# The RWKV-7 loop of a hybrid backbone, rewritten as a pipeline over units with TensorE in program order

## Chip, cores and metric

One core of a Trainium2 chip. The metric is the device time of one execution of the whole program in microseconds, the median of the runs. The program computes two layers; the change lies in the recurrent branch of the second one, in the last third of the time.

## What is computed

Odd layers mix tokens with a bidirectional RWKV-7 recurrence beside a Hyena convolution. For each of 8 heads a 64x64 state is carried over the 256 context tokens and then the 1024 latent ones, once forwards and once backwards; the two outputs are added, normalised per head, and given a bonus term.

```python
def step(s, inp):
    r_t, w_t, k_t, v_t, kk_t, b_t = inp
    sa = jnp.einsum('bhij,bhj->bhi', s, kk_t)
    s = s * w_t[:, :, None, :] - sa[..., None] * b_t[:, :, None, :] + v_t[..., None] * k_t[:, :, None, :]
    y = jnp.einsum('bhij,bhj->bhi', s, r_t) if emit else None
    return s, y
...
for d in range(2):
    s_ctx, yc = wkv_scan(s0, rc, decay_c, k_c, vc, kkc, b_c, reverse, ctx_out)
    _, yl = wkv_scan(s_ctx, r, decay_l, k_l, v, kk, b_l, reverse, True)
```

All operands are float32, and so are the products in the part that changes.

## The kernel before

The token loop is replaced by blocks of 64 tokens. A **job** is a pair of heads in one direction (4 pairs, 2 directions: 8 jobs). A job has 5 **units** of 256 tokens, the first of them context, so there are 40 units, taken in one order. In a unit there are 4 blocks of 64 tokens for each of 2 heads, and the work on one unit has these stages:

- the **front** (`rw_front`, L1462): loads, sums of log decays (`cs_ps`), exponentials, the keys `AKR` and `BK`, the Gram products `g_ps`, their masked parts `la` (the triangle to be inverted) and `gm` (the part for the outputs), transposes of the keys (`bk_ps`, evicted as `BT`) and the right-hand sides (`rh_ps`, evicted as `R`);
- the **inversion** of the 32x32 diagonal blocks of the triangles (`rw_invert`, L1569), one job at a time (the first job in two pieces) on VectorE: 31 steps of two instructions, `tmp<-L,X` and `X<-X,tmp`. `la` goes there through DRAM, and the result comes back as `XT`;
- the **solve** (`rw_solve`, L1599): three products of four 128x128 matmuls in a chain, `y_ps`, `z_ps`, `w_ps`, with an eviction behind each (`Z` on ScalarE, `R` on VectorE, `At` and `UV` on ScalarE);
- the **transitions** (`rw_trans`, L1629): 16 products of 64x64 (`ph_ps`), evicted by VectorE as `PH` and `RT`;
- the **scan** (`rw_scan`, L1653): 4 blocks one behind the other. Each adds `UV,BT` and the old state times `PH` in `st_ps`, evicts the new state `S` on ScalarE with the decay as its factor, copies the old state into a block-diagonal 128x128 tile, and makes outputs `yo_ps`;
- for the backward units with latent tokens, the bonus term and the **readout** (`rw_bonus`, `rw_readout`).

`rwkv` (L1370) goes through units b = 0 to 39. Fronts run up to 12 units ahead, solves two, transitions one. `PACE` sets how many inversion steps are traced between the others, at a high priority. The list of a loop turn is not the order in which engines work: the instructions are put in order for each engine by a scheduler, which may place any ready matmul on TensorE between two others. `Ordered` (L146) can make TensorE keep the order of the program; here it is off in this loop. From unit 28 on, `Final` projects the finished rows with the output weights (`fe_ps`), four of whose eight row blocks (4 to 7) come from the Hyena branch, and the weights are scaled and split into two parts when they are needed.

Of the kernel before, what the change touches and what calls it, by code (L numbers as in the profile page):

```python
# [10 lines left out]
F32 = mybir.dt.float32  # L11
# [18 lines left out]
def constants():  # L30
    c = {}
# [43 lines left out]
    gm[0, :, 0], gm[0, :, 1] = tc_ > sr, tc_ >= sr  # L75
    gm[1, :, 0], gm[1, :, 1] = tc_ < sr, tc_ <= sr
# [43 lines left out]
FB = 2  # L120
PB = (1, 1, 1, 1, 1)
# [7 lines left out]
PACE = (5,3,3,3)  # L129

NX = 3
XA = 0
# [41 lines left out]
class K:  # L174
# [879 lines left out]
    def gemm3(self, x):  # L1054
# [3 lines left out]
        with ExitStack() as st:  # L1058
# [175 lines left out]
            for n in range(4):  # L1234
                rw(n * 128, n, False, self.wnext(), 0)
                for _ in range(FG[n]):
                    self.rw_next_front()

    def rw_init(self):
# [3 lines left out]
        self.ep = self.fst.enter_context(tc.tile_pool(name="rwe", bufs=5, side="right", reuse_waits="tile"))  # L1243
# [3 lines left out]
        self.rpa = self.pst.enter_context(tc.tile_pool(name="rwpa", bufs=1, side="right", space=PSUM, reuse_waits="tile"))  # L1247
        self.jobs = [(j, d) for j in range(4) for d in range(2)]
        self.seq = [[0, 1, 2, 3, 4], [0, 4, 3, 2, 1]]
        self.fr, self.nf, self.inv = {}, 0, []  # L1250
        C = self.C = {}
        tri = fp.tile([128, 2, 256], F32, name="tri0", tag="kkf", bufs=2)
        nc.sync.dma_start(out=tri, in_=a["k_tri"].rearrange("d p k -> p d k"))
        C["tri"] = fp.tile([128, 2, 256], F32R, name="tri", bufs=1)
        nc.vector.tensor_copy(out=C["tri"], in_=tri)
        C["gm"] = fp.tile([128, 2, 128], F32, name="gm", bufs=1)
        nc.sync.dma_start(out=C["gm"], in_=a["k_gmask"].rearrange("d p k -> p d k"))
        C["LO"] = [[self.ep.tile([128, 4, 128], F32, name=f"LO0{i}", tag="LO0", bufs=5) for i in range(5)]]
        for t in C["LO"][0]:
            nc.vector.memset(t, 0.0)  # L1260
# [9 lines left out]
    def rw_inv(self, n):  # L1270
        while self.inv and n:
            n -= 1
            with self.tc.high_priority(1000):
                if next(self.inv[0], 1):
                    self.inv.pop(0)

    def rw_next_front(self):
        k, i = divmod(self.nf, 5)
        j, d = self.jobs[k]
        if i == 0:  # L1280
            self.fr[k] = self.rw_start(j, d, k)
        with self.tc.issue_after(self.table.ins):
            self.rw_front(self.fr[k], self.seq[d][i], *((self.ep, 5) if self.nf % 12 < 5 else (self.wp, 7)))
# [4 lines left out]
        self.nf += 1  # L1288
# [81 lines left out]
    def rwkv(self):  # L1370
        nc, tc, a = self.nc, self.tc, self.a
        with ExitStack() as st:
            kp = st.enter_context(tc.tile_pool(name="rwk", bufs=1, reuse_waits="tile"))
            pp = st.enter_context(tc.tile_pool(name="rwp", bufs=1, space=PSUM, reuse_waits="tile"))
            wp = st.enter_context(tc.tile_pool(name="rww", bufs=2, reuse_waits="tile"))
            self.rpb, self.wp = pp, wp
# [3 lines left out]
            for n, t in enumerate(C["XT"]):  # L1380
# [4 lines left out]
            C["LO"].append([kp.tile([128, 4, 128], F32, name=f"LO1{i}") for i in range(5)])  # L1385
            C["S"] = [kp.tile([128, 128], F32, name=f"S{i}") for i in range(4)]
            self.ns = 0
            jobs, seq, fr = self.jobs, self.seq, self.fr

            done = {"x": 0, "s": 0, "t": 0}  # L1390
            invert = self.rw_inv

            def fronts(n):
                while self.nf < min(n, 40):
                    invert(PACE[0])
                    self.rw_next_front()
                    if self.nf == 10:
                        for t in C["S"]:
                            nc.vector.memset(t, 0.0)

            def upto(what, n):
                while done[what] < min(n, 40):
                    m = done[what]
                    k, i = divmod(m, 5)
                    j, d = jobs[k]
                    q = seq[d][i]
                    if what == "x":
                        if i == 0:
                            invert(99)
# [747 lines left out]
```

## Time and profile before

| | us |
|---|---|
| median of 3 runs (2471.17 to 2472.86) | 2472.54 |
| the profiled execution | 2487.22 |
| its span, first to last instruction | 2485.4 |

The profile gives the time for which each engine was busy (PE is TensorE, DVE VectorE, ACT ScalarE, POOL GpSimd, SP the queue that issues DMAs), the granted TensorE clock, and rows for groups of instructions or for single runs of them in order of time. A line such as L158 can be that of a helper; the tiles' names tell which product is meant. Matmuls overlap, so the length of a matmul row includes a tail in which the next one of the same shape already runs. The shape before the operands' sizes, as in 64*64, is the part of the 128x128 array that an instruction uses. A float32 matmul stands in the trace as two instructions.

### The profile page before, as it was taken

What the parts mean: (1) busy time and instruction counts of PE and PEld (TensorE: products, weight loads), DVE (VectorE), ACT (ScalarE), POOL (GpSimd) and SP (SyncE); (2) the same over time, 40 slices, a digit from 0 to 9 for tenths busy, and PEclk for the clock granted to TensorE, in tenths of its full rate; (3) what the DMA queues carried; (4) which work ended last, traced back from release to release, by engine and by line L of the source; (5) the groups of instructions that cost most, each with busy time, mean ns of one, the idle gap of its engine ahead of it and who ended that gap; (6) DMA issues with size and microseconds to landing.
All of it is one profiled execution on the core that took longest, in us unless ns stands there. A gap on an engine that the chain in (4) does not pass through costs nothing. (4 is left out here: it accounts for less than half of the span.)

```text
span 2485.4 us, 45290 instructions
## 1 busy us (share of the span) xinstructions
PE 2275.4 (92%) x16647; PEld 1892.6 (76%) x16647; DVE 1568.8 (63%) x3175; ACT 1177.3 (47%) x2695; POOL 931.4 (37%) x959
## 2 busy tenths in 40 slices
PE   4999999999999989779899889999968999998997
PEld 3877888777878877668778778788757877887775
DVE  6255532368667867455486696457797776777425
ACT  5354434456556555532323221366435656665334
POOL 1253235201011654511033244224745464655512
PEclk8999999999999989889999999999858989999999
DMA  8433344682222766843454544574534343444522
GB/s 280 132 123 119 126 147 146 196 254 93 80 68 90 200 199 183 225 165 110 144 164 150 164 158 136 173 257 134 155 85 131 107 122 97 115 134 126 168 73 92
DMA packets 351428, 361.69 MB, mean 146 GB/s; under 512 B 83106, under 2 KB 283055, under 8 KB 350438
## 3 DMA queue, kind: packets, MB, share of 16 engines
q1 hardware_dynamic: 341894, 330.34, 43.5%
q10 hardware_dynamic: 9168, 24.25, 3.2%
q0 software_dynamic: 144, 4.19, 0.4%
q8 instruction: 132, 2.16, 0.4%
q14 instruction: 90, 0.74, 0.1%
HBM read 260.07 MB, written 100.10 MB: 145 GB/s over the span
## 5 line engine op out<-in xcount | busy, mean ns | idle before, releaser
L158 PE MATMUL g_ps<-xl,w_hi 128*128 128x512 f32 x1056 | 268.0, 399 | 1.0 <-ACT w_hi L192 1.0
L158 PEld LDWEIGHTS g_ps<-xl,w_hi 128*128 128x128 f32 x1056 | 198.9, 191 | 44.0 <-issue 1.9
L158 PE MATMUL s_ps<-k,q 128*128 128x256 f32 (+1 forms) x704 | 199.9, 381 | 7.6 <-DVE pn L700 4.3
L441 POOL TENSOR_TENSOR al_acc<-al_acc,al_t 128x512 f32<-128x512 f32 x98 | 129.0, 1316 | 185.6 <-ACT al_t L439 155.5
L196 DVE TENSOR_TENSOR w_lo<-w_raw,w_hi 128x256 fp32r<-128x256 f32 (+1 forms) x184 | 131.2, 769 | 86.6 <-PE g_ps L158 45.3
L187 ACT COPY pt<-pt_ps 128x512 f32<-128x512 f32 (+1 forms) x203 | 102.1, 506 | 139.3 <-PE pt_ps L161 133.7
L1586 DVE TENSOR_TENSOR tmp<-L,X 80x112 f32<-80x112 f32 (+25 forms) x279 | 136.4, 489 | 17.8 <-DMA L<-LD 8.9
L1588 DVE TENSOR_TENSOR X<-X,tmp 80x112 f32<-80x112 f32 (+25 forms) x279 | 140.6, 504 | 6.5
L158 PE MATMUL g_ps<-xl,w_lo 128*128 128x512 f32 x528 | 137.8, 395 | 0.0
L161 PE MATMUL pt_ps<-ident,p 128*128 128x128 f32 x704 | 118.1, 283 | 17.7 <-DVE pt L185 7.5
L158 PE MATMUL g_ps<-xhi,w_hi 128*128 128x512 f32 (+1 forms) x528 | 118.2, 366 | 8.9 <-DVE ac_res L283 4.7
L161 PEld LDWEIGHTS pt_ps<-ident,p 128*128 128x128 f32 x704 | 80.8, 141 | 52.9 <-DVE pt L185 14.8
L158 PEld LDWEIGHTS s_ps<-k,q 128*128 128x128 f32 x704 | 109.9, 200 | 14.6 <-DVE p L700 7.1
L695 ACT ACTIVATE p<-p,mn 128x1280 f32<-128x1280 f32 (+1 forms) x96 | 103.4, 1077 | 35.7 <-DVE p L700 35.5
L439 ACT ACTIVATE al_t<-al_w,condT 128x512 f32<-128x512 f32 x98 | 70.8, 722 | 101.7 <-POOL al_acc L441 60.9
L158 PE MATMUL g_ps<-xhi,w_lo 128*128 128x512 f32 (+1 forms) x528 | 118.2, 362 | 0.0
L881 POOL TENSOR_TENSOR bias<-namask,tt 128x384 f32<-128x384 f32 x64 | 67.5, 1055 | 125.9 <-DVE mn L890 52.0
L158 PEld LDWEIGHTS g_ps<-xl,w_lo 128*128 128x128 f32 x528 | 98.2, 188 | 21.1 <-issue 1.4
L158 PE MATMUL g_ps<-xlo,w_hi 128*128 128x512 f32 (+1 forms) x528 | 112.8, 356 | 0.0
L158 PEld LDWEIGHTS g_ps<-xhi,w_hi 128*128 128x128 f32 x528 | 90.0, 194 | 29.5 <-DVE qraw L549 5.4
L158 PE MATMUL g_ps<-AKR,BK 64*128 64x128 f32 (+1 forms) x640 | 91.1, 335 | 22.6 <-DVE AKR L1505 14.8
L158 PEld LDWEIGHTS g_ps<-xhi,w_lo 128*128 128x128 f32 x528 | 89.0, 189 | 18.9 <-issue 5.8
(438 smaller groups left out, 5869.4 us busy)
## 6 DMA issues: line engine op xcount, KB each, us to landing
w_raw<-rec_w_in SPq DMA_DIRECT2D x33, 512.0 KB
hfw<-FW SPq DMA_DIRECT2D x32, 512.0 KB
w_raw<-attn_w_in SPq DMA_DIRECT2D x13, 1024.0 KB
al_w<-rec_ada_w SPq DMA_DIRECT2D x48, 256.0 KB
tt<-TG SPq DMA_DIRECT2D x64, 192.0 KB
kkf<-KK SPq DMA_DIRECT2D x40, 256.0 KB
q<-qb SPq DMA_DIRECT2D x64, 128.0 KB
HS<-hs SPq DMA_DIRECT2D x32, 256.0 KB
```

Of the source, the lines that this page charges most:

```text
L158: return self.keep(self.pe.matmul(*args, **kw))
L161: return self.keep(self.pe.transpose(*args, **kw))
L187: self.nc.scalar.copy(out=out, in_=in_)
L196: e.tensor_tensor(out=lo, in0=full, in1=hi.bitcast(F32), op=ALU.subtract)
L439: nc.scalar.activation(out=o, in_=wt, func=AF.Copy, scale=self.condT[:, k, ci:ci + 1])
L441: nc.gpsimd.tensor_tensor(out=t, in0=t, in1=o, op=ALU.add)
L695: self.nc.scalar.activation(out=p, in_=p, func=AF.Exp, bias=mn, scale=-1.0, accum_out=rs)
L881: nc.gpsimd.tensor_tensor(out=b, in0=mask, in1=tt, op=ALU.subtract)
L1586: nc.vector.tensor_tensor(out=tv, in0=L[:, s:s + 1, rt].to_broadcast([n, nj, nt]), in1=X[:, rj, s:s + 1].to_broadcast([n, nj, nt]), op=ALU ...
L1588: nc.vector.tensor_tensor(out=X[:, rj, rt], in0=X[:, rj, rt], in1=tv, op=ALU.subtract)
```

## The change

The loop of `rwkv` is written anew, over b = -4 to 39, and `nc.tensor.on = True` keeps TensorE in program order inside it. In turn b, TensorE first works with 128x128 tiles on five different units: the third product of unit b+1 (`rw_solved`), the second of b+2, the first of b+3, then the sums of a front, the key transposes of the front before, and those of unit b+4. Then it works with 64x64 tiles: the four scan steps of unit b, with the halves of a Gram product and the right-hand sides of unit b+4 between the steps; the bonus sum, the transitions of b+1, the readout. Last come the products of `UV` for unit b+1 (`rw_own`), on 128*64 tiles, which now fill the bank `sy_ps` ahead of the scan. The three products of a solve stand in three turns.

Further edits: the Gram products use four 64x64 tiles in place of 64*128 ones; outputs and states are kept as rows of head and token, so the block-diagonal copy of the state is gone, `Y` has another layout, and the bonus and readout products are 64x64; `la` and `gm` become one tile `LG`, masked by two VectorE instructions of 512 elements a row (GpSimd's masking and ScalarE's copy are gone); `AKR` is made by one exponential and one product of 512; of GpSimd's work in a front, one step goes to ScalarE (`kd`) and two products go to VectorE (`kd`, `BK`); LO tiles are filled late, four in all; four PSUM banks rotate for everything but `ph_ps` (two) and `sy_ps` (two); inversion steps have a high priority only ahead of the loop; loads of a front come a turn earlier. `Final` takes its tiles from other places, and its products stand in program order at the end of a turn.

In the order of TensorE this shows within one unit. Before, a stretch of 12 out of 28 rows from one `w_ps` to the next:

```order
L158 MATMUL w_ps<-R,XT_17606 128x128 x4
L161 MATMUL bk_ps<-ident,BK 128x128 x4
L158 MATMUL st_ps<-UV,BT 64x64 x2
L158 MATMUL st_ps<-S,PH 64x64 x2
L161 MATMUL rh_ps<-ident,AKR 128x2x64 x2
L158 MATMUL rh_ps<-V,la 64x64 x8
L158 MATMUL ph_ps<-BT,At 64x64 x2
L158 MATMUL ph_ps<-gm,At 64x64 x2
L158 MATMUL ph_ps<-BT,At 64x64 x2
L158 MATMUL ph_ps<-gm,At 64x64 x2
L158 MATMUL y_ps<-R,XT_17604 128x128 x4
L158 MATMUL cs_ps<-tri,sgs 128x256 x4
```

Now, from one `w_ps` on, the first 12 rows of a turn in the middle of the loop:

```order
L157 MATMUL w_ps<-R,XT_17506 128x128 x4
L157 MATMUL z_ps<-Z,LO_17507 128x128 x4
L157 MATMUL y_ps<-R,XT_17504 128x128 x4
L157 MATMUL cs_ps<-tri,sgs 128x256 x4
L160 MATMUL bk_ps<-ident,BK 128x128 x4
L160 MATMUL rh_ps<-ident,AKR 128x2x64 x2
L157 MATMUL sy_ps<-S,PH 64x64 x2
L157 MATMUL sy_ps<-S,RT 64x64 x2
L157 MATMUL g_ps<-AKR,BK 64x128 x8
L157 MATMUL sy_ps<-S,PH 64x64 x2
L157 MATMUL sy_ps<-S,RT 64x64 x2
L157 MATMUL g_ps<-AKR,BK 64x128 x8
```

The scan steps stood singly between products of other shapes; they now stand together, behind one run of 128x128 products.

On VectorE the inversion steps stand differently against the other work. `R<-R,z_ps` comes once a unit. Before, a stretch between two of them, in the fourth job's inversion:

```order
L1620 TENSOR_TENSOR R<-R,z_ps 128x512
L1649 TENSOR_TENSOR PH<-ident_17610,ph_ps 128x2x2x64
L1651 TENSOR_TENSOR RT<-AKR,ph_ps 128x2x2x64
L1534 TENSOR_TENSOR la<-g_ps,gm 128x256 x2
L1515 TENSOR_TENSOR BK<-af,E 128x2x2x64
L1506 TENSOR_TENSOR AKR<-AKR,kkf 128x2x128
L1586 TENSOR_TENSOR tmp<-L,X 80x31
L1588 TENSOR_TENSOR X<-X,tmp 80x31
L1586 TENSOR_TENSOR tmp<-L,X 80x60
L1588 TENSOR_TENSOR X<-X,tmp 80x2x30
L1620 TENSOR_TENSOR R<-R,z_ps 128x512
```

Now the start of the unit whose first eight steps stand behind `RT` (one step is shown of the eight):

```order
L1697 TENSOR_TENSOR R<-R,z_ps 128x512
L1562 TENSOR_TENSOR BK<-kd,E 128x2x128
L1563 TENSOR_TENSOR BK<-af,E 128x2x2x64
L1554 TENSOR_TENSOR AKR<-AKR,kkr 128x2x128
L1557 TENSOR_TENSOR kd<-kd,kkr 128x256
L1597 TENSOR_TENSOR LG<-g_ps,gm 128x512 x2
L1738 TENSOR_TENSOR PH<-ident_17519,ph_ps 128x2x2x64
L1740 TENSOR_TENSOR RT<-AKR,ph_ps 128x2x2x64
L1655 TENSOR_TENSOR tmp<-L,X 80x31
L1657 TENSOR_TENSOR X<-X,tmp 80x31
```

Before, the 31 steps of a job are spread over four or five units. Now they stand in three units out of five: counted from one `R<-R,z_ps` to the next, ten units hold 8, 16, 7, 0, 0, 10, 15, 6, 0 and 0 steps (62, two jobs), and the products `BK` and `kd` stand behind `R`.

On ScalarE, the copy of the keys `BT` now stands ahead of the first state of a unit:

```order
L1538 ACTIVATE E<-cs_ps 128x256
L1541 ACTIVATE AKR<-cs_ps 128x512
L1545 ACTIVATE Dt<-cs_ps 128x4
L191 CAST sgs<-sg 128x256
L1574 COPY BT<-bk_ps 128x512
L1775 ACTIVATE S<-sy_ps,Dt 128x64
L1556 ACTIVATE kd<-af,oka,vec 128x256
L1775 ACTIVATE S<-sy_ps,Dt 128x64 x2
L1636 COPY R<-rh_ps 128x512
L1775 ACTIVATE S<-sy_ps,Dt 128x64
```

Before, twelve ScalarE instructions of a scan (four evictions and eight copies of half a state) stood between those of other stages.

The diff, cut to what matters here:

```diff
-FB = 2
-PB = (1, 1, 1, 1, 1)
+BANKS = ({"f": 3}, {"f": 4, "p": 1, "y": 2})
-PACE = (5,3,3,3)
-NX = 3
-XA = 0
+PACE = (5, 2, 2, 4)
+NX = 4
+SETS = (5, 8)
...
-    def rw_inv(self, n):
+    def rw_inv(self, n, first=False):
         while self.inv and n:
             n -= 1
-            with self.tc.high_priority(1000):
+            with self.tc.high_priority(1000) if first else ExitStack():
...
+            whole, late = None, None
+            self.rw_inverses(0)
+            self.rw_vectors(0)
+            nc.tensor.on = True
+            for b in range(-4, 40):
+                step, vg = [None] * 4, None
+                if at(b) is not None:
+                    k, i, q = self.rw_unit(b)
+                    j, d = self.jobs[k]
...
+                    step = list(self.rw_scan(b, Y))
+                if at(b + 5) is not None:
+                    self.rw_vectors(b + 5)
+                if at(b + 1) is not None:
+                    self.rw_solved(b + 1)
+                if at(b + 2) is not None:
+                    self.rw_second(b + 2)
+                if at(b + 3) is not None:
+                    self.rw_first(b + 3)
+                if late:
+                    self.rw_stats(*late)
+                self.rw_inv(PACE[1])
+                old, whole = whole, None
+                if self.nl < 40:
+                    self.rw_next_load()
+                if self.nf < 40:
+                    whole = self.rw_next_front()
...
+                    self.rw_turned(self.fr[ko], qo, *pool)
+                    fill = self.rw_gram(self.fr[ko], qo, *pool)
+                if at(b + 4) is not None:
+                    self.rw_keys_turned(b + 4)
+                self.rw_inv(PACE[2])
+                for s in range(4):
+                    if step[s]:
+                        step[s]()
+                    if s < 2:
+                        next(fill, None)
+                    if s == 2 and at(b + 4) is not None:
+                        self.rw_right(b + 4)
...
+                if at(b + 1) is not None:
+                    self.rw_trans(b + 1)
+                if late:
+                    self.rw_readout(*late)
...
+                if b >= 0:
+                    self.rw_outputs(b, Y)
+                self.rw_inv(PACE[3])
+                if at(b + 1) is not None:
+                    self.rw_own(b + 1)
+                if at(b + 4) is not None and b > -4:
+                    self.rw_inverses(b + 4)
...
+                if b >= 28:
+                    F.after(b)
...
+        if lat:
+            nc.vector.tensor_tensor(out=AKR, in0=AKR, in1=kkr[:, 0:2].rearrange("p a (i t) -> p i a t", t=128), op=ALU.mult)
+        else:
+            nc.vector.tensor_tensor(out=AKR[:, :, 1, :], in0=AKR[:, :, 1, :], in1=kv, op=ALU.mult)
-        nc.gpsimd.tensor_scalar(out=kd, in0=v3(af), scalar1=self.col("rwkv_k_a", j), scalar2=C["oka"][:, j:j + 1],
-                                op0=ALU.mult, op1=ALU.add)
-        nc.gpsimd.tensor_tensor(out=kd, in0=kd, in1=kf, op=ALU.mult)
+        nc.scalar.activation(out=kd, in_=v3(af), func=AF.Identity, scale=self.col("rwkv_k_a", j), bias=C["oka"][:, j:j + 1])
+        nc.vector.tensor_tensor(out=kd, in0=kd, in1=kf, op=ALU.mult)
+        nc.vector.tensor_tensor(out=BK[:, :, 64:192], in0=kd, in1=E, op=ALU.mult)
-        self.last_bk = nc.gpsimd.tensor_tensor(out=BK[:, :, 64:192], in0=kd, in1=E, op=ALU.mult)
...
+    def rw_gram(self, F, q, wp, bufs):
+        gp = [self.rps([128, 4, 128], "g_ps") for h in range(2)]
+        for ci in range(4):
+            i, c = divmod(ci, 2)
+            zc = slice(64 * c, 64 * c + 64)
+            for m in range(2):
+                for h in range(2):
+                    z, zo, f0 = slice(64 * h, 64 * h + 64), slice(64 * m, 64 * m + 64), 128 * c + 64 * m
+                    nc.tensor.matmul(gp[h][zo, ci, c0:128], BK[z, i, f0:f0 + 64],
+                                     AKR[z, i, :, zc] if q > 0 else AKR[z, i, 1, zc], start=True, stop=True,
+                                     tile_position=(64 * h, 64 * m))
+            if ci == 1:
+                yield
+        for h in range(2):
+            nc.vector.tensor_tensor(out=LG[:, h, :, c0:128], in0=gp[h][:, :, c0:128],
+                                    in1=mask.unsqueeze(1).to_broadcast([128, 4, 128 - c0]), op=ALU.mult)
...
+    def rw_own(self, n):
+        sy = G["sy"] = self.rps([128, 2, 4, 64], "sy_ps", "y")
+        for ci in range(4):
+            i, c = divmod(ci, 2)
+            for part in range(2 if q > 0 else 1):
+                for h in range(2):
+                    zo = slice(64 * h, 64 * h + 64)
+                    nc.tensor.matmul(sy[zo, part, ci, :], LG[:, h, ci, 0:64] if part else BT[:, ci, zo], UV[:, i, c, h, :],
+                                     start=(ci == 0 and part == 0), stop=False, skip_group_check=True, tile_position=(0, 64 * h))
...
+        def step(ci):
+            i, c = divmod(ci, 2)
+            sy, PH, RT, S = G["sy"], G["PH"], G["RT"], F["S"]
+            if S is not None:
+                for h, zo in heads:
+                    nc.tensor.matmul(sy[zo, 0, ci, :], PH[zo, i, c, :], S[zo], start=False, stop=True, skip_group_check=True,
+                                     tile_position=(64 * h, 64 * h))
+            t = F["S"] = wp.tile([128, 64], F32, name="S", bufs=4)
+            with self.tc.high_priority(60):
+                nc.scalar.activation(out=t, in_=sy[:, 0, ci, :], func=AF.Copy, scale=Dt[:, n0 + ci:n0 + ci + 1])
+            if q > 0:
+                for h, zo in heads:
+                    nc.tensor.matmul(sy[zo, 1, ci, :], RT[zo, i, c, :], S[zo], start=False, stop=True, skip_group_check=True,
+                                     tile_position=(64 * h, 64 * h))
-                for h, zo in heads:
-                    nc.scalar.copy(out=sd[zo, zo], in_=S[zo])
-                nc.tensor.matmul(yp[zc, i, :], RT[:, i, c, :], sd, start=True, stop=False, tile_position=(0, 64 * c))
```

## Rows read from the trace of the kernel before

**Rows 1.** The page: busy time of each engine over the span.

```profile
PE 2275.4 (92%) x16647; PEld 1892.6 (76%) x16647; DVE 1568.8 (63%) x3175; ACT 1177.3 (47%) x2695; POOL 931.4 (37%) x959
```

**Rows 2.** Busy time in stretches; columns: window, length, each engine, clock, DMA.

```profile
core 0: us, PE busy (x) PEld busy (x) DVE busy (x) ACT busy (x) POOL busy (x), PEclk, DMA share, GB/s
1902.30:2255.80 353.50, 341.20 (x3853) 286.62 (x3852) 263.17 (x614) 228.25 (x755) 200.98 (x287) 0.93 0.41 113
2255.80:2455.00 199.20, 190.96 (x1577) 150.19 (x1578) 98.17 (x200) 82.72 (x258) 76.84 (x98) 0.95 0.42 124
1775.00:1860.00 85.00, 61.66 (x418) 50.69 (x415) 77.03 (x163) 36.40 (x112) 50.53 (x63) 0.59 0.37 101
```

**Rows 3.** Timeline of TensorE in one unit: start, length, product, count.

```profile
2201.93 0.33 PE L158 MATMUL st_ps<-S,PH 64*64 64x64 f32 x4
2202.20 0.94 PE L158 MATMUL y_ps<-R,XT 128*128 128x128 f32 x6
...
2205.83 1.16 PE L158 MATMUL z_ps<-Z,LO 128*128 128x128 f32 x8
...
2217.20 0.45 PE L158 MATMUL ph_ps<-BT,At 64*64 64x64 f32 x12
...
2220.91 1.71 PE L158 MATMUL g_ps<-AKR,BK 64*128 64x128 f32 x16
```

**Rows 4.** Groups on ScalarE from 1902.3 to 2255.8: count, busy us, mean ns, idle before.

```profile
L1674 ACT ACTIVATE S<-st_ps,Dt 128x64 f32<-128x64 f32 x105 | 33.2, 316 | 25.9 <-PE st_ps L158 24.1
...
L1554 ACT COPY BT<-bk_ps 128x512 f32<-128x512 f32 x26 | 15.2, 585 | 2.3 <-PE bk_ps L161 0.9 <-PE st_ps L158 0.9
```

**Rows 5.** Groups on VectorE in the same stretch.

```profile
L1588 DVE TENSOR_TENSOR X<-X,tmp 80x231 f32<-80x231 f32 (+15 forms) x166 | 81.8, 493 | 3.5
L1586 DVE TENSOR_TENSOR tmp<-L,X 80x87 f32<-80x87 f32 (+15 forms) x165 | 78.2, 474 | 8.6 <-DMA L<-LD 5.5
L1534 DVE TENSOR_TENSOR la<-g_ps,gm 128x256 f32<-128x256 f32 x50 | 20.7, 415 | 8.0 <-PE g_ps L158 6.6 <-DMA iok<-KK 1.1
L1620 DVE TENSOR_TENSOR R<-R,z_ps 128x512 f32<-128x512 f32 x27 | 18.3, 677 | 9.2 <-PE z_ps L158 9.2
L1515 DVE TENSOR_TENSOR BK<-af,E 128x256 f32<-128x256 f32 x26 | 13.9, 534 | 35.3 <-ACT E L1490 35.3
...
L1649 DVE TENSOR_TENSOR PH<-ident,ph_ps 128x256 f32<-128x256 f32 x27 | 11.1, 410 | 2.0 <-PE ph_ps L158 2.0
```

**Rows 6.** Groups on GpSimd in the same stretch.

```profile
L1538 POOL TENSOR_TENSOR gm<-gm 128x256 f32<-128x256 f32 x42 | 33.7, 804 | 27.4 <-ACT gm L1537 26.6 <-DMA ioa<-AS 0.8
L1517 POOL TENSOR_TENSOR BK<-kd,E 128x256 f32<-128x256 f32 x26 | 26.0, 1001 | 68.4 <-ACT E L1490 38.9 <-issue 27.7 <-PE st_ps L158 1.6
L1508 POOL TENSOR_SCALAR kd<-af,vec,oka 128x256 f32<-128x256 f32 x25 | 22.8, 910 | 1.4
L1510 POOL TENSOR_TENSOR kd<-kd,kkf 128x256 f32<-128x256 f32 x25 | 20.7, 826 | 0.4
```

**Rows 7.** Timeline of VectorE: two inversion instructions with GpSimd idle, then two beside it.

```profile
2101.11 0.37 DVE L1588 TENSOR_TENSOR X<-X,tmp 80x207 f32<-80x207 f32 x1
2101.52 0.35 DVE L1586 TENSOR_TENSOR tmp<-L,X 80x192 f32<-80x192 f32 x1
...
2184.56 0.68 DVE L1588 TENSOR_TENSOR X<-X,tmp 80x112 f32<-80x112 f32 x1
...
2187.47 0.64 DVE L1586 TENSOR_TENSOR tmp<-L,X 80x31 f32<-80x31 f32 x1
```

**Rows 8.** Two idle times of TensorE in its timeline (in brackets, with the releaser).

```profile
2020.71 0.34 PE L158 MATMUL st_ps<-UV,BT 128*64 128x64 f32 x4 [0.65 <-ACT S L1674]
...
2022.96 1.44 PE L158 MATMUL w_ps<-R,XT 128*128 128x128 f32 x5 [1.66 <-DVE R L1620]
```

**Rows 9.** Busy time in the stretches around them, columns as in rows 2.

```profile
2012.00:2022.30 10.30, 8.32 (x110) 6.48 (x110) 10.14 (x25) 7.13 (x23) 6.40 (x10) 1.00 0.38 98
2022.30:2036.00 13.70, 13.04 (x80) 10.99 (x80) 10.78 (x23) 6.07 (x18) 8.25 (x15) 0.50 0.42 118
```

More of the change, by code (lines that the diff above doesn't have):

```diff
@@ L1287, in rw_next_front, with rw_whole @@
             next(self.inv[0])
-        self.nf += 1
+    def rw_whole(self):
+        self.rw_next_load()
+        n, pool = self.rw_next_front()
+        k, i, q = self.rw_unit(n)
+        with self.tc.issue_after(self.table.ins):
+            for _ in self.rw_gram(self.fr[k], q, *pool):
+                pass
+            self.rw_turned(self.fr[k], q, *pool)
+        self.rw_ready(n)
     def rw_pre(self, sp):
@@ L1608, in rw_solve @@
             nc.sync.dma_start(out=UV[64 * (1 - c):64 * (1 - c) + 64, :, c], in_=vsrc[c])
[L1610 to L1622 removed]
+        ps = self.rw_prod(self.C["XT"][n % NX], G.pop("R"), "w_ps")
+        At = G["At"] = wp.tile([128, 4, 64], F32, name="At", bufs=1)
         nc.scalar.copy(out=At, in_=ps[:, :, 0:64])
@@ new lines, in step, with rw_outputs @@
+            if q > 0:
+                for h, zo in heads:
+                    nc.tensor.matmul(sy[zo, 1, ci, :], RT[zo, i, c, :], S[zo], start=False, stop=True, skip_group_check=True,
+                                     tile_position=(64 * h, 64 * h))
+        return [lambda ci=ci: step(ci) for ci in (range(4) if d == 0 else range(3, -1, -1))]
+    def rw_outputs(self, n, Y):
+        k, _, q = self.rw_unit(n)
+        F = self.fr[k]
+        G = F["g"].pop(q)
+        if q > 0:
+            yv = Y[:, 4 * q - 4:4 * q, :]
+            if F["d"] == 0:
+                self.nc.scalar.copy(out=yv, in_=G["sy"][:, 1])
@@ L2025, in take, with pair @@
         return pool.tile(list(shape), dt, name="f" + tag, tag=tag,
-                         bufs=1 if tag in "LX" else 5 if pool is self.k.ep else 7)
+                         bufs=1 if tag in "LX" else SETS[0] if pool is self.k.ep else SETS[1])
+    def pair(self, pool, dt=F32R):
+        t = self.take(pool, "LG", dt, (128, 2, 512))
+        return [t[:, i] for i in range(2)]
     def weights(self, k, tiles):
@@ L2094, in after @@
         if b == 28:
-            self.raws = [take(wp, "gm", F32) for _ in range(2)]
+            self.raws = self.pair(ep, F32)
             self.gate1 = [take(ep, t, F32) for t in ("AKR", "BT")]
```

424 lines of the change are left out of this document (203 added, 221 removed).

## The prediction, made before the changed kernel ran

> **What bounds the kernel now.** The page gives TensorE 92% of the span and VectorE 63% [rows 1], but the change lies in the last third, so the next view is busy time by stretches. In the middle of the loop, from 1902.3 to 2255.8 us, TensorE is busy for 341.2 of 353.5 us, VectorE for 263.2, ScalarE for 228.3 and GpSimd for 201.0 [rows 2]. ScalarE evicts 105 states there, four a unit [rows 4]: 26 units, **13.6 us each**, of which TensorE fills 13.1. It is the bound because the scheduler always finds a ready matmul; how much of the 13.1 is work is seen in its timeline [rows 3]. Eight instructions of `z_ps` show 1.16 us, six of `y_ps` 0.94, so one costs 0.11 and a run ends with some 0.28 of tail. Twelve of `ph_ps` show 0.45, some 0.02 each and a tail of 0.2. But `y_ps` starts 0.27 after the four `S,PH`, which at 0.02 would have needed 0.08: a change of shape costs nearly 0.2. And 16 of `g_ps`, which use one half of the rows at a time, show 1.71.
>
> The next engine is VectorE. Inversion steps take 160.0 of its 263.2 us, 0.97 for a pair [rows 5], which leaves 4.0 us a unit for the rest. The pair isn't one price: with GpSimd idle the two take 0.37 and 0.35, 0.76 with the gaps, beside GpSimd's work 0.68 and 0.64, some 1.33 [rows 7].
>
> **TensorE's work.** Three products of eight instructions in one run are 24 x 0.11 plus a tail, 2.9 us. For `cs_ps`, `bk_ps` and the transposes of `rh_ps` I put ten such instructions, 1.1. The 80 small instructions of transitions, scan and right-hand sides are 80 x 0.02 and a tail or two, 2.0; the Gram products, now on both halves, 1.1 in place of 1.7 [rows 3]; the products of `UV` 0.9, the readout 0.4 in the mean, four changes of shape with what they drain 0.1 each. That is **8.5 us** for 13.1; if TensorE stayed the bound and full, the loop would lose 4.6 x 26, some 120 us.
>
> It can't stay full, since in program order nothing ready may jump ahead. A scan step needs `S,PH` (0.33), ScalarE's eviction (0.316) [rows 3, 4] and the hand-overs; only the `RT` products and half a Gram product stand beside it. The first state's eviction stands behind the copy `BT` (0.585) [rows 4]. `bk_ps` waits for `R` (0.677) and two `BK` products of about 0.53 [rows 5], while TensorE has `y_ps` and `cs_ps`, some 1.5. I take 1.5 us a unit (from 0.5, if the fill covers a step, to 3): **10.0 for a unit without inversion steps**.
>
> **VectorE's work.** GpSimd gives up the masking of `gm` (33.7), one `BK` product (26.0) and both steps of `kd` (22.8 and 20.7), 103 of its 201 us [rows 6]: its share falls from 57% to 28%. Between 0.72 for a pair with GpSimd idle [rows 7] and 0.97 at 57% [rows 5], 28% gives 0.84; with the gaps I take 0.80 where no readout is made and 0.94 in units with one, of which GpSimd keeps its part. VectorE gains two `LG` of 512 at some 0.68 (as `R` [rows 5]) for two `la` of 0.415, 0.5; one `BK` and one `kd`, 0.5 each; it saves some 0.3 as `AKR` needs one product: 4.0 + 1.2 = 5.2 a unit. With 62 pairs in ten units, 52 + 31 x 0.80 + 31 x 0.94 = 106: a floor of 10.6 a unit, below the 13.6 of today.
>
> **Where the two meet.** The order on VectorE puts the 62 pairs of ten units into six of them. There the two engines take turns: TensorE stops at `bk_ps` until VectorE has done its pairs, `R` and `BK`, and VectorE then stops at `PH` until TensorE has been through keys, scan and Gram products. Of the 10.0 us, `bk_ps` to `ph_ps` is 5.0 (10.0 less 2.9 + 0.7 ahead of it and 1.4 behind); with `PH` and what must follow of it 0.7, `R` 0.6 and `BK` 0.75 that is 7.05 in series, and the pairs come on top. Ten units: 4 x 10.0 + 6 x 7.05 + 31 x 0.80 + 31 x 0.94 = **136 us**, again 13.6 a unit. Some pairs stand between `LG` and `PH` and are hidden; some readout instructions are not counted; I let these cancel.
>
> **The clock.** Waits of TensorE cost twice. After idle times of 0.65 and 1.66 us [rows 8] the granted clock was 0.50, its 1.2 GHz level, from 2022.3 to 2036.0, with TensorE busy for 13.0 of 13.7 us [rows 9]: some 6.5 us of it was lost. The new order has waits of 5 us and more in the step units. I put one such fall in ten units where TensorE's work bounds, 7 us: 143 in ten, 14.3 a unit, and 0.7 x 26 = **+18 us** (bounds: 0.3 to 1.4 a unit, +8 to +36).
>
> The Trainium skill ("TensorE: Matmul & The Clock Gate", section "A second HAM failure mode: psum-queue depth-cycling") says that TensorE's short idles between groups of matmuls make its clock swing between the levels. By that rule taken to its end, the loop would stay at the low level (third rival).
>
> **Ends of the loop.** From 1775 to 1860 VectorE is busy for 77.0 of 85.0 us with the first inversions, GpSimd for 50.5 [rows 2]. Two pieces of 31 pairs run there; with GpSimd's share halved each saves some 0.2, -12 us. Three turns more in the pipeline cost about +5: **-7** (-12 to 0). From 2255.8 on, `Final` fills TensorE, 191.0 of 199.2 us [rows 2]. Fronts and solves are mostly over there, so of the saving about 1 us a unit remains, against the 1.5 of waits that the projection, now last in each turn, doesn't fill: 12 x 0.5 = **+6** (from -6 to +20, where the first projection also waits for the weights that GpSimd scales).
>
> **Sum.** -7 + 18 + 6 = +17 on the profiled 2487.2, 2504. That execution is 14.7 above the median, so the forecast is **2490 us**. VectorE in step units takes over what TensorE gives up.
>
> **Rival 1, faster.** GpSimd leaves VectorE nearly alone during the pairs, and the clock holds. The place is again the step units; the price 0.76 a pair [rows 7], so 62 x 0.76 = 47 in place of 54, and four pairs of 0.76 hidden beside the scan: 126 for ten units, 12.6 each, -26 us; with -12 at the start and 0 in the tail 2434.5, **2435**. It decides from a pair below 0.8 us in units with readout, and a granted clock as now (0.93) or above. For it: half of GpSimd's work goes. Against: the readout keeps it busy where half the pairs stand, and waits of over a microsecond were followed by a fall [rows 8, 9].
>
> **Rival 2, no change.** The bound moves to VectorE at the same price: 13.5 a unit, -3, -7 and +6 at the ends, **2468 to 2475**, put at 2471. The order shows the change doing what it says, so only a coincidence of prices leads here.
>
> **Rival 3, cold.** Each turn's wait lets the clock fall, and it stays at 0.5. A unit without pairs then takes 15.5 in place of 10.0, since most of its products double; the others hide it: 158 for ten, 15.8 each, +57; the tail +20; **2550**. Against it: in the step units the work before the wait is dense.
>
> **Rival 4, the changes of shape are the whole price.** Once they are gone, VectorE's floor of 10.6 less the contention (52 + 47 = 99 for ten, 9.9) and the 10.0 of a light unit set the time: 10.2, -88, with -12 at the start **2372**. The nearly 0.2 for a change speaks for it, TensorE's and VectorE's taking turns against. The Trainium skill ("TensorEngine Tiling (Array Packing)", section Key Properties) says that a change of the tiling mode drains TensorE; by it alone the sum would come out here.
>
> **How the numbers follow.** Forecast 0.42 (13.9 to 15 a unit: 2478 to 2515 is its own range); rival 1 0.34; rival 2 0.12; rival 3 0.08; rival 4 0.04. About 0.2%, 5 us, is what a measurement of this kernel can tell from no change. Faster: 0.34 + 0.04 = 0.38; same 0.12; slower 0.42 + 0.08 = 0.50. The range takes in rival 1 down to 2428, the forecast and half-way to rival 3, 2540; what is left out is rival 4, most of rival 3 and the fast tail of rival 1, some 0.17.
>
> **What would show it.** In the profile after, from the first state to the 28th unit: TensorE below 75% busy, its idle put down to VectorE at `bk_ps` (`BK`) and to ScalarE's `S`; VectorE at 75 to 80%, GpSimd near 30%; units with steps of 15 to 22 us and light ones near 10. A mean pair near 0.76 to 0.80 everywhere and a clock of 0.93 would be rival 1; a granted clock near 0.6 rival 3; step units as short as the light ones rival 4. The forecast is wrong if VectorE's pairs run beside the scan rather than in turn with it, or if light units wait more than 3 us.

## The result, and the profile after

The changed kernel takes **2608.2 us** (median of 4 runs, 2605.3 to 2609.1) beside 2472.7 before (4 runs, 2471.2 to 2480.9): 1.0539 times as long, 95% interval 1.0515 to 1.0563. The forecast was 2490, its range ended at 2540. The profiled execution has a span of 2607.3 and lies 0.9 above the median; the one before lay 14.5 above its own, so the profiles show 121.9 of the 135.5 us.

The stretch from the second unit's first state to the 28th's is 26 units, before (1895.8 to 2249.9; [rows 2] begins 6.5 us later) and after (1902.0 to 2334.7). Busy time in stretches after the change, the loop, what follows, and the first inversions, columns as in [rows 2]:

```profile
1902.00:2334.70 432.70, 299.86 (x4524) 264.13 (x4524) 253.31 (x636) 175.22 (x491) 93.18 (x156) 0.73 0.33 89
2334.70:2607.30 272.60, 190.28 (x2052) 157.00 (x2052) 114.08 (x244) 82.68 (x228) 86.91 (x115) 0.86 0.36 109
1775.00:1860.00 85.00, 33.88 (x350) 27.93 (x347) 72.85 (x169) 21.85 (x56) 22.57 (x27) 0.60 0.39 109
```

The same two stretches before:

```profile
1895.80:2249.90 354.10, 341.86 (x3851) 287.59 (x3852) 267.18 (x625) 227.10 (x751) 200.67 (x282) 0.93 0.42 116
2249.90:2485.40 235.50, 212.38 (x1709) 165.93 (x1707) 117.42 (x244) 100.23 (x311) 87.67 (x117) 0.94 0.39 118
```

The start is 6.2 us later, the loop 78.6 longer (16.6 us a unit for 13.6), the end 37.1: 121.9, the difference of the spans. In the loop TensorE is idle for 132.8 us, before for 12.2, and its mean granted clock is 0.73 for 0.93. VectorE, for which the forecast named 75 to 80%, is busy for 59% only. The waits of TensorE in the loop after the change (what waited, for what, us in all, times, longest):

```profile
PE sy_ps L157 <- ACT S L1775: 53.5, 86, 1.6
PE rh_ps L160 <- DVE R L1697: 38.1, 14, 7.3
PE bk_ps L160 <- ACT UV L1715: 36.8, 8, 8.3
PE y_ps L157 <- DMA XT<-XD: 3.7, 1, 3.7
```

The first of them is 2.1 us a unit, more by itself than the 1.5 that the forecast put for all waits of a unit without inversion steps, and 84 of its 86 stand ahead of `S,RT`. TensorE's timeline of one scan step and a half, after the change, at a granted clock of 0.50:

```profile
2022.11 0.48 PE L157 MATMUL sy_ps<-S,PH 64*64 64x64 f32 x4
2023.01 0.37 PE L157 MATMUL sy_ps<-S,RT 64*64 64x64 f32 x2 [0.41 <-ACT S L1775]
2023.03 0.37 PE L157 MATMUL g_ps<-AKR,BK 64*64 64x64 f32 x2
2023.17 0.32 PE L157 MATMUL sy_ps<-S,RT 64*64 64x64 f32 x2
2023.19 0.72 PE L157 MATMUL g_ps<-AKR,BK 64*64 64x64 f32 x14
2023.70 0.43 PE L157 MATMUL sy_ps<-S,PH 64*64 64x64 f32 x4
2024.54 0.37 PE L157 MATMUL sy_ps<-S,RT 64*64 64x64 f32 x2 [0.41 <-ACT S L1775]
```

`S,RT` multiplies the old state, which has long been there. It waits for the eviction of the *new* one, which reads other columns of the same bank `sy_ps`. With the wait ahead of `S,RT`, the half Gram product behind it can't fill the eviction's time either, and by the time of the next `S,PH` nothing is left to wait for.

### The profile page after: what moved, and what is told of

It is laid out like the page before. It is cut to its first block, busy times and chain, and to the rows that moved or that the text cites. A ratio compares the mean times of both kernels' runs of the same rounds, so it can differ in the third digit from the quotient of the medians.

```text
span 2607.3 us, 47090 instructions
## 1 busy us (share of the span) xinstructions
PE 2179.3 (84%) x17799; PEld 1834.0 (70%) x17799; DVE 1555.9 (60%) x3211; ACT 1098.6 (42%) x2303; POOL 781.1 (30%) x778
## 5 line engine op out<-in xcount | busy, mean ns | idle before, releaser
L157 PE MATMUL sy_ps<-S,RT 64*64 64x64 f32 x512 | 53.9, 301 | 105.8 <-ACT S L1775 105.8
L1655 DVE TENSOR_TENSOR tmp<-L,X 80x112 f32<-80x112 f32 (+25 forms) x279 | 110.8, 397 | 41.2 <-DMA L<-LD 34.1
L157 PEld LDWEIGHTS sy_ps<-S,RT 64*64 64x64 f32 x512 | 32.3, 173 | 126.9 <-ACT S L1775 126.9
L1657 DVE TENSOR_TENSOR X<-X,tmp 80x112 f32<-80x112 f32 (+25 forms) x279 | 113.3, 406 | 7.8 <-DVE tmp L1655 0.3
L157 PE MATMUL g_ps<-AKR,BK 64*64 64x128 f32 (+1 forms) x1280 | 75.8, 352 | 43.9 <-DVE AKR L1552 36.1
```

Source lines behind the costliest of these rows:

```text
L157: return self.keep(self.pe.matmul(*args, **kw))
L1655: nc.vector.tensor_tensor(out=tv, in0=L[:, s:s + 1, rt].to_broadcast([n, nj, nt]), in1=X[:, rj, s:s + 1].to_broadcast([n, nj, nt]), op=ALU ...
L1657: nc.vector.tensor_tensor(out=X[:, rj, rt], in0=X[:, rj, rt], in1=tv, op=ALU.subtract)
```

## The experiments

All ratios are to the kernel before, run beside each on the same chip. "Loop" is the stretch from the second unit's first state to the 28th's in the profile, "clock" the mean granted clock there. 0.01 of ratio is 25 us. no_steps, rt_nosteps, rt_nostats and rt_plain leave work out: they show what that work costs where it stands, and are no way to compute the result.

| kernel | us | ratio (95%) | loop, us | clock |
|---|---|---|---|---|
| the change | 2608.2 | 1.0539 (1.0515 to 1.0563) | 432.7 | 0.73 |
| order_off | 2505.1 | 1.0086 (1.0057 to 1.0115) | 350.1 | 0.86 |
| rt_first | 2524.8 | 1.0178 (1.0136 to 1.0219) | 364.5 | 0.83 |
| io7 | 2600.6 | 1.0480 (1.0423 to 1.0537) | 433.2 | 0.74 |
| no_steps | 2563.1 | 1.0324 (1.0285 to 1.0363) | 383.1 | 0.79 |
| rt_free | 2493.0 | 1.0052 (1.0025 to 1.0078) | 349.2 | 0.87 |
| rt_gate | 2529.4 | 1.0208 (1.0177 to 1.0239) | 371.6 | 0.82 |
| rt_tail | 2537.1 | 1.0232 (1.0203 to 1.0261) | 366.5 | 0.84 |
| rt_both | 2528.5 | 1.0197 (1.0171 to 1.0224) | 371.4 | 0.83 |
| sep_bank | 2528.4 | 1.0184 (1.0152 to 1.0216) | 362.7 | 0.84 |
| rt_nosteps | 2474.5 | 0.9978 (0.9960 to 0.9996) | 318.7 | 0.88 |
| rt_free_hp | 2491.7 | 1.0034 (1.0015 to 1.0053) | 348.8 | 0.86 |
| rt_final | 2516.5 | 1.0150 (1.0115 to 1.0184) | 364.1 | 0.84 |
| rt_depth | 2546.0 | 1.0264 (1.0237 to 1.0291) | 371.7 | 0.85 |
| rt_depth_free | 2480.7 | 1.0000 (0.9982 to 1.0018) | 340.7 | 0.88 |
| rt_depth_both | 2563.5 | 1.0330 (1.0304 to 1.0356) | 379.9 | 0.84 |
| rt_nostats | 2475.8 | 0.9984 (0.9969 to 0.9999) | 344.8 | 0.84 |
| rt_plain | 2417.3 | 0.9756 (0.9726 to 0.9785) | 284.5 | 0.90 |
| depth_free_hp | 2489.0 | 1.0040 (1.0026 to 1.0055) | 350.0 | 0.87 |

### The wait for the bank

Two edits take this wait away in different ways. In rt_first the products are issued ahead of the eviction:

```diff
+            if q > 0:
+                for h, zo in heads:
+                    nc.tensor.matmul(sy[zo, 1, ci, :], RT[zo, i, c, :], S[zo], ...)
             with self.tc.high_priority(60):
                 nc.scalar.activation(out=t, in_=sy[:, 0, ci, :], func=AF.Copy, ...)
-            if q > 0:
-                for h, zo in heads:
-                    nc.tensor.matmul(sy[zo, 1, ci, :], RT[zo, i, c, :], S[zo], ...)
```

> In a scan step the two products S,RT are issued ahead of the eviction of the new state and no longer behind it. They need the old state alone, but write the bank that the eviction reads, and in the changed kernel they wait for it 86 times, 53.5 us in all between units 1 and 28. TensorE's order stays word for word. Theory A, this wait is a third of the loss: half a Gram product now stands between the eviction and the next S,PH, so 25 to 40 us of waits go, and the clock gives back as much again: 2540 to 2575. Theory B, the eviction is on the path of the scan anyway and the wait moves to S,PH in full: 2595 to 2612.

In sep_bank they stay behind it, but outputs have a bank of their own:

```diff
-BANKS = ({"f": 3}, {"f": 4, "p": 1, "y": 2})
+BANKS = ({"f": 3}, {"f": 4, "p": 1, "y": 1, "o": 1})
...
-        sy = G["sy"] = self.rps([128, 2, 4, 64], "sy_ps", "y")
+        two = G["sy"] = (self.rps([128, 4, 64], "sy_ps", "y"), self.rps([128, 4, 64], "so_ps", "o") if q > 0 else None)
```

> The changed kernel with state and outputs of a unit in a PSUM bank each (one buffer apiece in place of two shared ones); S,RT stays behind the eviction in the program. Theory A, TensorE waits at S,RT only because the eviction reads the bank that S,RT writes: the wait of 53.5 us goes as it does with S,RT issued first, 2505 to 2545. Theory B, it is the place behind the eviction in the program that costs, whatever the bank: 2590 or more.

Theory A holds in both, and for rt_first with more than it expected: 3.6% and 3.55% of the time, some 88 us, two thirds of the loss. In sep_bank, where `S,RT` stays behind the eviction in the program, the wait for `S` is this:

```profile
PE sy_ps L157 <- ACT S L1775: 8.4, 13, 2.6
```

The edit of rt_first moves an instruction of ScalarE only, so TensorE's program order is the same. Its timeline there, again at 0.50:

```profile
2000.00 0.48 PE L157 MATMUL sy_ps<-S,PH 64*64 64x64 f32 x4
2000.27 0.31 PE L157 MATMUL sy_ps<-S,RT 64*64 64x64 f32 x1
...
2000.44 0.68 PE L157 MATMUL g_ps<-AKR,BK 64*64 64x64 f32 x14
2001.11 0.48 PE L157 MATMUL sy_ps<-S,PH 64*64 64x64 f32 x4
```

A step takes 1.11 us in place of 1.59, with no idle time. The waits of TensorE in the loop of rt_first, and its busy time there:

```profile
PE rh_ps L160 <- DVE R L1697: 44.5, 17, 9.3
PE bk_ps L160 <- ACT UV L1715: 30.9, 5, 9.8
PE sy_ps L157 <- ACT S L1779: 10.8, 22, 2.4
```

```profile
1900.10:2264.60 364.50, 257.00 (x4536) 226.24 (x4532) 247.70 (x637) 174.02 (x490) 94.66 (x156) 0.83 0.39 105
```

The wait itself fell from 53.5 to 10.8, and TensorE's whole idle time from 132.8 to 107.5, 25 us less. But its *busy* time fell as well, for the same products: from 299.9 to 257.0, 43 us, with the clock at 0.83 for 0.73. Of the loop's 68 us the larger part came through the clock: TensorE was busy at the low level of 1.2 GHz for 172 us of the loop after the change and for 80 in rt_first.

### TensorE's program order

order_off has this edit, rt_free has it with `S,RT` first:

```diff
             self.rw_vectors(0)
-            nc.tensor.on = True
```

> The changed kernel without TensorE's program order: the scheduler may put any ready matmul between two others again, every other edit stays. Theory A, TensorE's fixed order is what costs: its idle time between unit 1 and 28 (132.8 us of 432.7) goes back to 15 to 40 us, the granted clock rises from 0.73 to over 0.9, and the time falls from 2608 to 2420 to 2480. Theory B, the waits come from the other edits (the work moved onto VectorE, the loads of the bonus, the shared banks): at least half of the idle time stays, and the time is 2540 or more.

> Both earlier edits together: S,RT ahead of the eviction, and TensorE without program order. Theory A, the two edits remove the same waits (without the fixed order the scheduler filled the wait for the eviction, 17.8 us of it were left in that run between units 1 and 28): 2485 to 2505, little under the 2505 of the run without order. Theory B, they remove different waits and add up: 2505 - 83 = 2422, at least under 2460.

order_off lies between its two theories: 4.5% (112 us) come back, but idle time stays at 70 of 350 us, over half of the 132.8, and the clock at 0.86. rt_free answers as theory A: without the order the bank's wait costs 0.3%, hardly more than the intervals, and with it 3.6%. That another product fills it there fits the waits for `S`, 17.8 us in order_off for 53.5. With `S,RT` first the order still costs 1.3%, some 31 us. rt_final frees only the projection:

```diff
                 if b >= 28:
+                    nc.tensor.on = False
                     F.after(b)
+                    nc.tensor.on = True
```

> S,RT ahead of the eviction, and the projection at the end of each of the last turns without program order (the rest of the loop keeps it). With the order everywhere the stretch from unit 28 on is 260 us, without it anywhere 239, before the change 236. Theory A, the projection could fill the waits of the last units: 20 us less, 2500 to 2510. Theory B, the waits there are those of the fixed order of the rest: within 6 us of 2525.

It gains 0.3%, within its interval and between its two theories, and the stretch from unit 28 on falls from 260.0 to 246.1 us in the profile; with no order at all (rt_free) it is 238.5.

### VectorE's steps, the readout, and the queues

no_steps and rt_nosteps (with `S,RT` first) have the first of these edits, rt_nostats (with `S,RT` first) the others, rt_plain all:

```diff
-        for s in (range(31) if d == 0 else range(31, 0, -1)):
+        for s in ((range(31) if d == 0 else range(31, 0, -1)) if F["k"] == 0 else ((0,) if d == 0 else (31,))):
...
-        nc.gpsimd.memset(X.rearrange("p j t -> p (j t)")[:, 0::33], 1.0)
+        if F["k"] == 0:
+            nc.gpsimd.memset(X.rearrange("p j t -> p (j t)")[:, 0::33], 1.0)
```

```diff
     def rw_bonus(self, j, q):
...
-        for n, src in (("k", ...), ("a", ...), ("b", ...), ("r", ...), ("v", ...), ("g", ...)):
+        for n, src in (("v", ...), ("g", ...)):
...
+        return io[0], io[1], None
...
     def rw_bonus_sum(self, late):
+        return
...
     def rw_stats(self, j, q, Y, vg):
+        return
```

> The inversion of all jobs but the first is left out but for one step of its 31 (its diagonal is left at zero), so that the loop has no inversion work on VectorE. Theory A (the step of the forecast), TensorE and VectorE take turns on the steps, some 54 us of pairs in ten units and 140 us in 26 units: without them the time falls by 110 us or more, below 2500. Theory B, the steps fill waits of VectorE and only those ahead of R cost (TensorE waits 38.1 us for R between units 1 and 28): 2540 to 2575.

> S,RT ahead of the eviction, and the inversion of all jobs but the first left out but for one of its 31 steps (its diagonal left at zero). Theory A, once the bank's wait is gone the inversion sets the pace (its steps on VectorE and the two ways through DRAM): ten units fall from 145 us to 110 or less, and the time from 2525 to 2440 or below. Theory B, the fixed order with its waits for ScalarE and the clock sets it: the gain stays what it was with the bank's wait, 45 us, 2470 to 2490.

> S,RT ahead of the eviction, and the statistics of the readout and the bonus sum with its loads left out (outputs go through the transposes, the scaling and the store unnormalised). Theory A, the queues are held up by the readout's chain over four engines (VectorE to ScalarE to GpSimd to VectorE, and its late loads) in the units that have one: these fall from 17 to 23 us to 12 to 15, ten units from 143 to 120 to 128, the time to 2450 to 2480. Theory B, the inversion alone holds those units: ten units 135 or more, 2505 or more.

> The same, and the inversion of all jobs but the first left out but for one step (its diagonal at zero): what is left is TensorE's fixed order with the fronts, solves, transitions and scans. Theory A (the forecast's sum), a unit without steps takes some 10.0 us: ten units 95 to 108, the stretch from unit 1 to 28 under 280 us, the time under 2430. Theory B, the order's own waits keep a unit at 12 or more: 2450 or more.

The steps are worth 2.2% with the bank's wait and 2.0% without it, some 50 us: theory B in both, far from the 110 that the forecast's taking turns would have given. The readout is worth 1.9% as well, and both together 4.2%. What is left then is close to the pipeline as the forecast had counted it. Busy time in the loop of rt_plain, then in two units of rt_first without steps:

```profile
1896.30:2180.80 284.50, 235.31 (x4490) 208.39 (x4492) 116.79 (x254) 165.84 (x465) 59.49 (x73) 0.90 0.45 119
```

```profile
1920.60:1930.00 9.40, 8.89 (x192) 7.75 (x184) 3.15 (x6) 6.27 (x18) 1.60 (x4) 1.00 0.52 140
1967.90:1977.90 10.00, 8.69 (x178) 7.49 (x178) 6.29 (x16) 6.54 (x21) 3.75 (x10) 1.00 0.39 101
```

10.9 us a unit in the mean of rt_plain, just above its theory A (under 280 us), and units of 9.4 and 10.0 where nothing is late.

Then single instructions that hold up a queue: io7, rt_gate, rt_tail (its generator `end` is the readout from the sum with the bonus on), and rt_both, which has the last two.

```diff
-            t = wp.tile([128, 256], F32, name=f"io{n}", tag="iovg" if n in "vg" else "io", bufs=4)
+            t = wp.tile([128, 256], F32, name=f"io{n}", tag="iovg" if n in "vg" else "io", bufs=4 if n in "vg" else 7)
```

```diff
-                self.rw_inv(PACE[1])
+                with self.tc.issue_after(self.last_r.ins) if at(b + 2) is not None else ExitStack():
+                    self.rw_inv(PACE[1])
...
-                self.rw_inv(PACE[3])
+                if not fresh:
+                    self.rw_inv(PACE[3])
```

```diff
-                if late:
-                    self.rw_stats(*late)
+                with self.tc.issue_after(self.last_uv.ins) if at(b + 1) is not None else ExitStack():
+                    next(end, None)
+                    end = iter(())
+                    if late:
+                        self.rw_stats(*late)
```

> Seven buffers in place of four for the bonus loads, so that those of the next unit don't wait until the last ones are used up. Theory A, late loads hold up whole queues: in the changed kernel VectorE idles 27 us and GpSimd 60 us for them between units 1 and 28, the readout's cast stands behind that on ScalarE and At behind the cast, so that TensorE waits 36.8 us at bk_ps. These go: 2555 to 2580. Theory B, At waits for the chain of the readout however early the loads are: 2598 to 2612.

> S,RT ahead of the eviction, and a job's inversion steps are held back: none in the turn of its last Gram product, and those of the next turns behind that turn's R on VectorE. Theory A, what is left of the loss in the kernel with S,RT first is VectorE's queue: steps wait for their load L 39.9 us with R behind them, and TensorE waits 44.5 us for R. With that gone and the clock higher: 2455 to 2490. Theory B, the steps delay something else then (XT comes later, y_ps waits for it): 2510 or more.

> S,RT ahead of the eviction, and the last part of a readout (from its sum with the bonus to the cast and the store) as well as the statistics are issued behind At and UV of the next turn on ScalarE and behind them in the program elsewhere. Theory A, TensorE's 30.9 us of waits at bk_ps are At and UV standing behind the readout's cast, which waits for GpSimd 35.8 us: 2480 to 2505. Theory B, the wait passes to the next instruction of ScalarE's queue: 2515 to 2530.

> S,RT ahead of the eviction, steps held back and the readout's end moved. Theory A, queues in which a late instruction holds up a punctual one are the whole of what is left, and TensorE's idle time between units 1 and 28 falls from 107 to under 50 us with the clock at 0.9 or more: 2400 to 2450, faster than before. Theory B, the fixed order finds the next wait (the loop can't go below some 13 us a unit): 2470 or more.

Theory A fails each time: io7's gain of 0.6% lies within the intervals, rt_gate and rt_both are level with rt_first, and rt_tail is slower than its theory B, 0.5% above rt_first, where the intervals just overlap. The waits move. TensorE's longest ones in rt_tail, then in rt_both:

```profile
PE rh_ps L160 <- DVE R L1705: 83.0, 16, 14.0
PE sy_ps L157 <- ACT S L1787: 16.2, 23, 5.1
```

```profile
PE rh_ps L160 <- DVE R L1710: 48.5, 16, 5.0
PE y_ps L157 <- DMA XT<-XD: 40.9, 6, 7.6
```

Where the readout no longer stood ahead of `At`, the wait at `bk_ps` is gone from the list and the one for `R` has nearly doubled; where steps began later, `XT` came late. VectorE in rt_first shows the head of such a queue, the first step of a job, which waits 9.67 us for its load while `R` stands behind it:

```profile
2123.97 0.42 DVE L1859 TENSOR_TENSOR yo<-yo,iov 128x256 f32<-128x256 f32 x1
2134.05 0.28 DVE L1655 TENSOR_TENSOR tmp<-L,X 80x31 f32<-80x31 f32 x1 [9.67 <-DMA L<-LD]
```

Behind that stands SP's queue, in which the store of the last `LG` was issued at 2127.38, six us after `LG` was done, behind other transfers, and the load of `L` at 2130.62. I then took it that the inversion's way through five turns sets the pace, and gave it six:

```diff
-                if at(b + 2) is not None:
-                    self.rw_second(b + 2)
-                if at(b + 3) is not None:
-                    self.rw_first(b + 3)
+                if at(b + 2) is not None:
+                    self.rw_first(b + 2)
...
+                if at(b + 2) is not None:
+                    self.rw_second(b + 2)
                 if at(b + 1) is not None:
                     self.rw_own(b + 1)
-                if at(b + 4) is not None and b > -4:
-                    self.rw_inverses(b + 4)
+                if at(b + 3) is not None and b > -3:
+                    self.rw_inverses(b + 3)
```

> S,RT ahead of the eviction, and y_ps of a unit one turn later (its z_ps stands behind the transitions of the same turn), so that a job's inversion has six turns from its last Gram product to its first y_ps in place of five. Theory A, the inversion's way (LG through DRAM to L, 31 steps, X through DRAM to XT) is what a job of five units can't be shorter than, 140 to 146 us for ten units in nearly every kernel with inversion: ten units fall to 120 to 130, and the time from 2525 to 2455 to 2490. Theory B, the turns are held up by single late instructions at the head of a queue, whatever the depth: 2515 or more.

> The same depth without TensorE's program order. Theory A (the inversion's way sets the pace in both): 2430 to 2465, faster than before. Theory B, without the order TensorE already filled these waits: 2485 to 2500, as the kernel without the depth (2493).

> The same depth with the order, and the readout's end issued behind At and UV. Theory A, with the inversion's wait gone the place of the readout on ScalarE counts, which it didn't before: 15 to 30 us less than the kernel with the depth alone. Theory B, as in the kernel without the depth it only moves the wait from bk_ps to R: within 10 us of it, or above.

In rt_free_hp the steps have `with self.tc.high_priority(1000):` throughout; depth_free_hp has that, the depth and the seven buffers, and no order.

> S,RT ahead of the eviction, TensorE without program order, and the inversion steps with a high priority in the whole loop, as they had before the change. Theory A, the inversion sets the pace of what is left, so steps taken up as soon as they can be shorten it: 2450 to 2480, level with the kernel before or faster. Theory B, the place of the steps doesn't matter while TensorE is free to fill: 2485 to 2500, as without the priority (2493).

> The fastest of the kernels with S,RT first (TensorE free, y_ps one turn later, 2481 beside 2480 before the change), with a high priority for the inversion steps and seven buffers for the bonus loads. Theory A, the inversion's way still bounds its units, and steps taken up at once shorten it: 2455 to 2472, faster than before. Theory B, 2475 to 2490, level with it.

That theory fell: rt_depth is slower than rt_first by 0.9%. rt_depth_both, which also holds the steps back as rt_gate does, is slower by another 0.7%. TensorE's wait for `XT` is gone from its list, and the first two there are now these:

```profile
PE sy_ps L157 <- ACT S L1779: 60.0, 41, 8.9
PE w_ps L157 <- DVE R L1697: 33.3, 16, 6.3
```

Without the order the depth is worth 0.5% and brings the kernel level with the one before; a priority for the steps adds nothing that can be measured (rt_free_hp), and with the depth and more buffers the kernel is 0.4% slower than without the two (depth_free_hp), beyond the intervals. No version of those that compute everything beats the kernel before.

## Why the prediction was wrong

The direction was right, the size was not: 135 us for 17. In the profiles it is 121.9 for 17, and of the 105 between them 61 lie in the loop (78.6 for 18), 31 at the end and 13 at the start.

- **The term of the clock failed.** One fall in ten units, 7 us, was counted, 18 us in the loop. In the trace 234 of the loop's 432.7 us are at the low level, with TensorE busy for 172 of them; before it was 48 with 46, in rt_first 123 with 80. From the change to rt_first, 92 us less of busy time at the low level made the busy time 43 us shorter. At that price, an estimate, the clock cost some 80 us of the changed kernel's loop, 62 more than forecast: the loop's whole excess. The unit without steps in the last section, forecast at 10.0, took 15.3, 2.9 of them waiting. That is rival 3's mechanism and nearly its price (15.5); it had 0.08, and the forecast set it aside because the work ahead of the long waits is dense. But the short waits of the scan step make the larger part: with them gone the clock is 0.83, with 75 us of waits for `R` and `UV` still there. What is left up to 0.93 goes with those and is not taken apart.
- **Behind it stands the scan step.** The forecast wrote that the `RT` products and half a Gram product stand beside the eviction. They stand behind it: the order shown ahead of the prediction names no waits, and in the trace the first `S,RT` of a step waits for ScalarE, in all but two of 86 waits of 0.4 to 1.6 us. The Trainium skill has the rule ("PSUM — Partial Sum Buffer", section "PSUM bank collisions raise a hardware error"): the compiler's back end adds a dependency between any two instructions on different engines that touch the same bank in the same 32-partition quadrant, whatever the columns. By that rule `S,RT` waits for the eviction; the trace agrees (53.5 us of waits), and so does sep_bank, where the banks differ (8.4 us).
- **The sum of the waits was right by luck.** The forecast's ten units hold 51 us of waits, 133 in the loop; measured are 132.8, 5.1 us a unit. But 39 of the 133 were for the scan, `BT` and `bk_ps` of every unit, and the scan's wait for `S` alone is 53.5; 94 were for taking turns, and the waits for `R`, `UV` and `XT` are 79.
- **TensorE's work was right**: 8.5 us a unit, 10.0 with its waits, for 8.7 to 8.9 and 9.4 to 10.0 measured in units of rt_first. (The parts that the forecast lists add up to 8.8.) At the price above, an estimate, the work in the loop was 321 us before, 245 in order_off and 220 after the change: 3.9 us a unit were saved for 4.6 forecast, about 1 of them by the order, and lost again to waits and clock.
- **The pair of steps was too dear.** Its price fell to rival 1's, 0.757 us for the 0.76 that it had:

```profile
L1657 DVE TENSOR_TENSOR X<-X,tmp 80x207 f32<-80x207 f32 (+15 forms) x164 | 62.4, 381 | 4.7 <-DVE tmp L1655 0.3
L1655 DVE TENSOR_TENSOR tmp<-L,X 80x207 f32<-80x207 f32 (+15 forms) x164 | 61.6, 376 | 27.2 <-DMA L<-LD 23.1
```

  Before it was 0.97 [rows 5]. GpSimd is busy for 22% (93.2 of 432.7), forecast 28%. Rival 1 got its price and not its time: the loss stood in TensorE's waits and clock.
- **Taking turns was there, but through waits that the sum didn't have.** The long units of rt_first took 13 to 24 us, forecast 15 to 22, and its loop 10 us more than before, forecast 18. But the steps are worth 50 us, not 110 and more: beside VectorE's work it is the late load of `L` and the readout's chain that hold its queue and ScalarE's. That the sum comes out near for rt_first is luck, by terms that were partly wrong.
- **Start and end.** The start became 6 us longer (forecast 7 shorter): VectorE's first inversions run with GpSimd busy for 27%, but the first state comes at 1880.3 for 1875.7; why is not shown. The end became 37 us longer (forecast 6, at most 20): with `S,RT` first 25, without the order 3 (238.5 for 235.5). So some 12 of it are the bank's wait and 22 the order, about 14 of these the projection's place.

What stays open: which of the late instructions is the first cause in program order. Each one moved let another take its place, and the store and load of `L` were not tried on another queue. Nor is it shown why rt_free and rt_depth_free, with less work for TensorE than before, are no faster: TensorE is idle for 72 us of the loop in rt_free.

## What to carry to other kernels

Before an engine is put into a fixed order, list for each of its instructions what it waits for, by bank and not by data: here a product that goes to a bank which is being read waited for the reader, and all behind it waited too. Issue everything that goes to a bank ahead of its eviction, or give it another bank. In the fixed order a short wait that came every turn cost more through the clock than by itself (43 us beside 25), and moving one late instruction or two gained nothing, as others took their place.

## What was not expected of the hardware

The same 4536 matmul instructions or so of the loop were busy for 299.9 us at a mean clock of 0.73 and for 257.0 at 0.83: 43 us, beside 25 of idle time that went. A unit without inversion steps shows it, with 178 instructions both times, first in the changed kernel and then in rt_first:

```profile
1984.40:1999.70 15.30, 12.39 (x178) 11.33 (x178) 6.44 (x15) 6.70 (x22) 2.89 (x8) 0.67 0.29 73
1967.90:1977.90 10.00, 8.69 (x178) 7.49 (x178) 6.29 (x16) 6.54 (x21) 3.75 (x10) 1.00 0.39 101
```

Elsewhere the changed kernel ran at the low level all the way from a unit's first state to that of the next (109 matmul instructions), behind a wait of 3.6 us and with waits of 0.5 to 0.9 us in it:

```profile
1959.90:1968.40 8.50, 6.33 (x109) 5.53 (x110) 6.02 (x19) 2.60 (x8) 0.93 (x1) 0.50 0.45 123
```
